# Two more raw weight tiles in a second MLP, an own first order for an attention layer, and a column copy moved three visits on

## The chip, the core and the metric

The kernel runs on one core of a Trainium2 chip. The core's engines work side by side and wait for one another through semaphores: TensorE (PE, matrix multiplies; loading a weight into it is counted apart as PEld), VectorE (DVE), ScalarE (ACT), GpSimd (POOL) and SyncE (SP), which here only issues DMAs. The metric is the device time of one execution in microseconds (us), lower is better.

## What is computed

Two transformer layers on 512 latent tokens and 256 context tokens of width 1024. Layer 0 mixes by differential attention, layer 1 by neighbourhood attention on an 8 x 64 grid plus the context; each is followed by an MLP of width 4096. Both halves of a layer are normed, and shifted, scaled and gated by vectors that come from conditioning vectors through a weight `w_mod`. Cut to what matters here:

```python
for i in range(DEPTH):                       # DEPTH = 2
    mod_l = split(silu(c) @ w_mod[i] + b_mod[i], 6)        # six sections of 1024, for latent tokens
    mod_c = split(silu(c_ctx) @ w_mod[i] + b_mod[i], 6)    # the same for context tokens
    h_l = rms_norm(x, norm1_g[i]) * (1 + mod_l[1]) + mod_l[0]
    h_c = rms_norm(ctx, norm1_g[i]) * (1 + mod_c[1]) + mod_c[0]
    y_l, y_c = mixer_i(h_l, h_c, ...)        # q, k, v projections, attention, output projection
    x = x + mod_l[2] * y_l
    x = x + mod_l[5] * (square(relu((rms_norm(x, norm2_g[i]) * (1 + mod_l[4]) + mod_l[3]) @ w_mlp1[i])) @ w_mlp2[i])
    ...
return x
```

Everything is float32. The last layer updates only the latent tokens.

## The kernel before

**Numbers in two parts.** Each float32 operand of a large product is split into a high part (ACT copies it to a reduced form) and the remainder (POOL or DVE subtracts, L152); a product is three multiplies, high by high, high by low, low by high. A weight is therefore loaded by SP into a raw tile of tag R (512 KB), ACT writes the high half of a tile of tag W from it (L146) and POOL the low half in two cuts (L152). The raw tile is free when both have read it.

**Tiles.** `sbt` (L81) hands out tiles by tag. For a tag in `self.room` it goes round over all places of the pools that are open for the tag: R has two places throughout, and two more are opened for the second MLP (L1208), four in all. There, R also takes the MLP's second weight in blocks (L887), some of which DVE adds or subtracts in place (L927 to L950), since the second MLP product is made of seven block products in place of eight.

**Who sets the order.** A planner places all instructions, at build time, by a clock of its own: an instruction goes to its engine's queue when, by that clock, what it needs is there, and among those that are ready the one that stands first in the program's text goes first. Inside `manual_schedule(engines=PINNED)` PE, SP and POOL (L61) keep the text's order among themselves; DVE and ACT are placed by the planner there too, but for single instructions that are held with `keep_in_program_order`. Each engine then works through its queue in order and waits where an input is not there.

**Layer 1's attention.** Eight groups of two heads. A group's steps are written out as a string of words, which `run` (L1074) goes through: `Q0a` to `Q5b` are halves of the projections of six token tiles (12 multiplies each, L414; tiles 0 and 1 are context), `U0`, `U2`, `U4` turn two tiles' queries and keys (transposes L640, L642), `S`, `T`, `V` are scores, turning and weighting of four units; `w` and `c` load and split the next group's weights; `m` is a visit, below. Marks behind a word (`'`) say that the step belongs to the group one or two back. Group 0 to 6 use CYCLE1 (L47); in group 0 the marked steps fall away, as there is no group behind it. The projections' sums lie in one of three PSUM banks of tag A (PS_ATTN1, L57), which ACT and DVE empty (L421, L626, L627).

**The seam in front of it.** The first MLP ends with `done0` (L1145), called for each of the six token tiles: it stores the tile, and after each odd tile norms the pair (`normed`, L310 to L316) and calls `modulated` (L319): for the eight slices of 128 columns, PE transposes both tiles (L333), ACT scales and shifts (L336), DVE writes the high and the low part (L338, L339) into `hT1`, from which the projections read. This lies outside the pinned region, before it in the text.

**Visits.** A section of the modulation is computed in four visits (`Mods.visit`, L1054; eight times two multiplies at L289, added up by DVE, L291), each with a weight of 1 MB which SP loads one visit ahead. The fourth visit stores the section's rows to DRAM (four ACT DMAs, L1068). For a shift or a scale of a norm (sections 0, 1, 3, 4) the next visit reads them back as columns, with two SP DMAs of 4 KB whose pieces are single numbers (L1060), and DVE writes them into `mB` (L276) or `mA` (L279) in `mod_set`. In the attention of layer 0 (the words of START0, CYCLE0 and END0) and in the first MLP it is the same routine.

## Time and profile before

| what | us |
|---|---|
| time before, median of three runs | 1849.92 (1848.83 to 1850.58) |
| the profiled execution's own time | 1851.53 |
| attention of layer 0, one turn of the written order | about 48 |
| first MLP, about | 558 to 1056 |
| the seam and the first group of layer 1 | 1056 to 1110 |
| attention of layer 1, projections of groups 1 to 7 | 1110 to 1410 |
| second MLP | 1480 to 1850 |

The kernel's page and the answers of its trace show all times from the start of the span. A row of a timeline gives start, duration, engine, line of the kernel, operation, the tiles written and read, how often, and in brackets the idle time in front and what ended it. Five lines of the page that the text below does not show again:

```profile
...
PE   6988999997899999999999988989998989999988
DVE  4677888876666565656559657768776567777685
POOL 3755666643335575766566613334445447878773
PEclk9989999998999999999999989999998989999999
...
PE 65%; DVE 11%; ACT 7%; POOL 6%; issue 5%; DMA 5%; ACTq 0%; SPq 0%; POOLq 0%; DVEq 0%
...
```

The slices are 46 us long each; slices 23 and 24 hold the seam, slices 33 and on the second MLP.

### The profile page before, as it was taken

The page shows a single profiled execution, that of the slowest core. Times are in us where ns is not written, and L with a number is a line of the kernel's source. Part 1 is how long each engine was busy: PE and PEld are TensorE (multiplying, and loading weights), DVE is VectorE, ACT ScalarE, POOL GpSimd, SP SyncE. Part 2 cuts the span into 40 slices and gives each one's busy share as a digit, 9 for nine tenths or more (in the row PEclk, how much of TensorE's full clock was granted, in tenths as well). Part 3 has the DMA queues.
Part 4 walks back from the last instruction along what each step waited for, and adds up shares of the span by engine and source line. Part 5 has one row for each costly group of instructions (what it writes and reads, how often), then busy time and mean ns, then how long its engine had stood idle before and what let it go on. Part 6 is the DMA issues. An engine that isn't in the chain of part 4 may idle for free.

```text
span 1849.7 us, 27540 instructions
## 1 busy us (share of the span) xinstructions
PE 1729.0 (93%) x9918; PEld 1521.2 (82%) x9918; DVE 1265.9 (68%) x2328; ACT 936.8 (51%) x1962; POOL 1046.2 (57%) x1002
## 2 busy tenths in 40 slices
PE   6988999997899999999999988989998989999988
PEld 4878888885788899899988878989897777878767
DVE  4677888876666565656559657768776567777685
ACT  4566776765344343334342446667676344544432
POOL 3755666643335575766566613334445447878773
PEclk9989999998999999999999989999998989999999
DMA  9222222225536644544442333333332333334441
GB/s 336 69 83 78 79 72 85 92 81 186 200 116 177 197 114 111 154 123 119 112 131 80 114 121 119 123 106 112 106 129 98 109 113 125 126 125 148 138 135 69
DMA packets 104809, 227.29 MB, mean 123 GB/s; under 512 B 22160, under 2 KB 38752, under 8 KB 100576
## 3 DMA queue, kind: packets, MB, share of 16 engines
q1 hardware_dynamic: 95152, 212.56, 36.1%
q10 hardware_dynamic: 9520, 12.97, 1.9%
q8 instruction: 78, 1.28, 0.3%
q14 instruction: 59, 0.48, 0.1%
HBM read 207.19 MB, written 18.30 MB: 122 GB/s over the span
## 4 chain that ended last, share of the span: by engine, by line
PE 65%; DVE 11%; ACT 7%; POOL 6%; issue 5%; DMA 5%; ACTq 0%; SPq 0%; POOLq 0%; DVEq 0%
PE PD L851 19%; PE PA L414 14%; PE PB L911 6%; PE PA L911 6%; PE PA L759 4%; POOL W L152 4%; PE PA L992 3%; DMA R<-in_w_dram 3%; PE PS L523 2%; PE PB L558 2%; PE PQ L404 1%; ACT W L146 1%; PE PS L662 1%; PE PB L708 1%; PE PB L693 1%
## 5 line engine op out<-in xcount | busy, mean ns | idle before, releaser
L152 POOL TENSOR_TENSOR W<-R,W 128x512 fp32r<-128x512 f32 x270 | 416.3, 1570 | 162.2 <-ACT W L146 161.4
L851 PE MATMUL PD<-Q,W 128*128 128x384 f32 (+2 forms) x1992 | 379.8, 344 | 11.7 <-DVE Q L339 5.6
L851 PEld LDWEIGHTS PD<-Q,W 128*128 128x128 f32 x1992 | 345.6, 189 | 35.0 <-ACT W L146 7.6
L146 ACT ACTIVATE W<-R 128x1024 fp32r<-128x1024 f32 (+1 forms) x165 | 168.0, 1021 | 189.9 <-DMA R<-in_w_dram 50.4
L152 POOL TENSOR_TENSOR W<-N,W 128x512 fp32r<-128x512 f32 x98 | 141.8, 1468 | 110.1 <-ACT W L146 103.8
L911 PE MATMUL PB<-W,H 128*128 128x512 f32 x738 | 191.9, 395 | 5.5 <-DVE Q L919 4.4
L911 PE MATMUL PA<-W,H 128*128 128x512 f32 x732 | 190.9, 395 | 3.8 <-DVE H L919 2.6
L414 PE MATMUL PA<-W,Q 128*128 128x384 f32 (+1 forms) x1008 | 175.8, 327 | 0.0
L911 PEld LDWEIGHTS PB<-W,H 128*128 128x128 f32 x738 | 139.5, 190 | 36.0 <-DVE Q L919 5.2
L301 POOL TENSOR_TENSOR SQ<-SQ,half 128x4 f32<-128x4 f32 (+1 forms) x96 | 95.3, 994 | 128.3 <-DVE SQ L427 127.1
L911 PEld LDWEIGHTS PA<-W,H 128*128 128x128 f32 x732 | 137.9, 189 | 34.6 <-DVE H L919 3.0
L414 PEld LDWEIGHTS PA<-W,Q 128*128 128x128 f32 x1008 | 159.9, 193 | 0.9
L414 PE MATMUL PA<-WB,H 128*128 128x384 f32 x576 | 108.7, 342 | 2.6 <-DVE Q L475 2.6
L146 ACT ACTIVATE W<-N 128x1024 fp32r<-128x1024 f32 x49 | 51.8, 1058 | 111.5 <-PE PB L911 39.4
L759 PE MATMUL PA<-W,H 128*128 128x512 f32 x384 | 98.5, 407 | 8.3 <-DVE T L764 3.8
L414 PEld LDWEIGHTS PA<-WB,H 128*128 128x128 f32 x576 | 98.7, 189 | 3.5 <-DVE Q L475 3.4
L869 DVE SCALAR_TENSOR_TENSOR H<-N,H 128x512 fp32r<-128x512 f32 (+1 forms) x57 | 67.2, 1181 | 47.1 <-ACT H L868 46.8
L851 PE MATMUL PD<-H,W 128*128 128x512 f32 (+1 forms) x408 | 95.2, 383 | 0.0
L759 PEld LDWEIGHTS PA<-W,H 128*128 128x128 f32 x384 | 72.1, 193 | 26.8 <-DVE T L764 5.9
L529 ACT ACTIVATE E<-PS,SA 128x768 f32<-128x768 f32 (+1 forms) x96 | 72.9, 759 | 40.4 <-DVE SA L528 36.9
L674 POOL TENSOR_SCALAR E<-E,SA 128x256 f32<-128x256 f32 x64 | 59.2, 936 | 55.8 <-DVE SA L671 55.4
L528 DVE TENSOR_REDUCE SA<-PS 128x1 f32<-128x768 f32 (+1 forms) x96 | 74.5, 777 | 21.3 <-ACT E L529 10.8
(265 smaller groups left out, 3540.0 us busy)
## 6 DMA issues: line engine op xcount, KB each, us to landing
R<-in_w_dram SPq DMA_DIRECT2D x121, 512.0 KB
M<-in_wmod_dram SPq DMA_DIRECT2D x32, 1024.0 KB
N<-in_w_dram SPq DMA_DIRECT2D x49, 512.0 KB
R<-in_wqa_dram SPq DMA_DIRECT2D x32, 384.0 KB
R<-in_wqb_dram SPq DMA_DIRECT2D x32, 384.0 KB
C<-in_wmod_dram SPq DMA_DIRECT2D x16, 512.0 KB
M<-in_wmod_dram SPq DMA_DIRECT2D x16, 512.0 KB
Y<-in_rpb_dram SPq DMA_DIRECT2D x48, 128.0 KB
```

Source lines behind the costliest of these rows:

```text
L146: high = nc.scalar.activation(w[:, 0, :n], raw, AF.Copy)
L152: low = (eng or nc.gpsimd).tensor_sub(w[:, 1, o:e], raw[:, o:e], w[:, 0, o:e].bitcast(F32))
L301: nc.gpsimd.tensor_tensor(r, ss, self.half[:, :n], op=ALU.pow)
L414: nc.tensor.matmul(acc[:, :n], hT[kt][:, x, P * i:P * i + P], w[kt // 2][:, y, o:o + n], start=(kt == 0 and p == 0), stop=(kt == KT - 1 an ...
L528: nc.vector.tensor_reduce(mx, s, op=ALU.max, axis=AX, negate=True)
L529: nc.scalar.activation(e[:, m, :nk], s, AF.Exp, bias=mx[:, 0:1], accum_out=sm[:, m:m + 1])
L674: nc.gpsimd.tensor_scalar_mul(e[:, 1, o:o + 256], e[:, 1, o:o + 256], r[:, 1:2])
L759: nc.tensor.matmul(ps, oHL[h][:, x, c:c + P], w[h // 2][:, y, 512 * (h % 2):512 * (h % 2) + 512], start=(first and h == hs[0] and p == 0), ...
L851: nc.tensor.matmul(ps[:, at:at + b1 - b0], w[kt // 4][:, x, o:o + P], hT[kt][:, y, b0:b1], start=(kt == 0 and p == 0), stop=(kt == KT - 1 ...
L869: nc.vector.scalar_tensor_tensor(u[:, 1], src, 1.0, u[:, 0].bitcast(F32), op0=ALU.mult, op1=ALU.subtract)
L911: nc.tensor.matmul(ps, u[:, x, f, P * i:P * i + P], w[:, y, 512 * f:512 * f + 512], start=(f == 0 and p == 0), stop=(f == 1 and p == 2))
L992: nc.tensor.matmul(ps, hd[:, x, P * i - c0:P * i - c0 + P], w[f][:, y, 512 * n:512 * n + 512], start=(f == 0 and p == 0), stop=(f == len(h ...
```

## The change

Three parts, which touch different stages.

- **Six raw tiles.** In the second MLP, tag R goes round over six places: the four of before and two tiles that lie idle there, one of tag C4 and one of tag X (`self.spare`, set once).
- **START1 and N.** `modulated` becomes a generator that stops in front of each further PSUM bank (four banks of two slices for this caller; `modulate` runs it through for the other). For the last pair of `done0` it is not run there; its four steps become the word N in a new order START1, which replaces CYCLE1 for group 0. In START1 the halves of Q0 and Q1 come first, then two N, Q2a, two N; the split `c0` and the load `w2` come after these, and the first visit `m` after Q3a.
- **Columns.** The two reads are issued one visit after the store, as before, into one constant tile `columns`; `mod_set` now stands at the head of the third visit after the store instead of the first.

```diff
--- before.py
+++ after.py
@@ -44,6 +44,7 @@
 END0 = """x0 x1 x2 x3 m S1' O2'' O3'' V4'' T0' U4' X0 V5'' T1' X1 m S2' O4'' X2 x4 V0' n S3' x5 P0a O5'' T2' X3 P1a
 X4 V1' O0' n S4' X5 B0 P0b V2' O1' x6 P1b T3' P2a T4' S5' P2b O2' P3a V3' V4' m P3b T5' P4a O3'
 X6 P4b V5' P5a P5b O4' O5'"""
+START1 = """w0 w1 Q0a Q0b Q1a Q1b N N Q2a N N c0 w2 Q2b U0 Q3a m Q3b c1 w3 Q4a Q4b c2 m U2 Q5a Q5b c3"""
 CYCLE1 = """w0 w1 Q0a m T3'' U4' Q1a c0 w2 V2'' V3'' Q0b S0' Q1b Q2a S1' Q2b Q3a T0' S2' Q4a c1 w3 T1' Q3b S3' V0' U0
 Q4b c2 m U2 Q5a T2' Q5b c3 V1'"""
 LAST1 = """Q0a m T3'' U4' Q1a c0 x0 x1 V2'' V3'' Q0b S0' Q1b X0 x2 Q2a S1' Q2b X1 Q3a T0' S2' Q4a T1' Q3b X2 S3' V0'
@@ -74,6 +75,7 @@
         self.dram = pool("dram", 1, space=DRAM)
         self.flip = 0
         self.room, self.turns, self.last = {"R": [(self.rpool, 2, None)]}, {}, {}
+        self.spare = {}
 
 
     BUFS = {"H": 8, "Q": 8, "E": 2, "X": 2, "Y": 6, "T": 1, "MA": 2, "SQ": 12, "SA": 12, "SO": 8, "C4": 1}
@@ -83,7 +85,10 @@
         if tag in self.room:
             pools = [r[:2] for r in self.room[tag] for _ in range(r[1])]
             k = self.turns[tag] = self.turns.get(tag, -1) + 1
-            pool, bufs = pools[k % len(pools)]
+            k %= len(pools) + len(self.spare.get(tag, ()))
+            if k >= len(pools):
+                return self.spare[tag][k - len(pools)]
+            pool, bufs = pools[k]
         else:
             pool, bufs = self.sb, self.BUFS[tag]
         return pool.tile(shape, dt, tag=tag, name=f"{tag}{self.n}", bufs=bufs)
@@ -197,6 +202,7 @@
 
         self.mA = c.tile([P, 2, 2, KT, 2], F32, name="mA")
         self.mB = c.tile([P, 2, 2, KT, 2], F32, name="mB")
+        self.columns = c.tile([P, KT, 2], F32, name="columns")
         self.rows = self.dram.tile([2, 6, 2, D], F32, name="rows")
 
     def load_layer0(self):
@@ -326,6 +332,8 @@
         bank = None
         for kt in range(KT):
             if kt % per == 0:
+                if kt:
+                    yield
                 bank = self.pst(tag[0], (P, 256 * per))
                 for k in range(kt, min(kt + per, KT)):
                     for j, xn in enumerate(xns):
@@ -337,6 +345,10 @@
                                  scale=self.mA[:, l, norm, kt, s:s + 1])
             nc.vector.tensor_copy(hT[kt][:, 0, cols], f)
             nc.vector.tensor_sub(hT[kt][:, 1, cols], f, hT[kt][:, 0, cols].bitcast(F32))
+
+    def modulate(self, *args):
+        for _ in self.modulated(*args):
+            pass
 
     def normed_early(self, xs):
 
@@ -813,7 +825,7 @@
                         nc.scalar.dma_start(self.x1[i][:, 512 * n:512 * n + 512], xh[i, n])
                 if i % 2 == 1:
                     xns = [self.normed([xh[j, 0], xh[j, 1]]) for j in (i - 1, i)]
-                    self.modulated(xns, (i - 1, i), l, 1, hT, tag_p)
+                    self.modulate(xns, (i - 1, i), l, 1, hT, tag_p)
 
         return dict(weights=weights, begin=begin, fetch=fetch, split=split, step=step, split_last=split_last, end=end)
 
@@ -1037,7 +1049,7 @@
 
 
     def __init__(self, b, todo, halves=()):
-        self.b, self.halves, self.ready, self.back = b, halves, [], []
+        self.b, self.halves, self.ready, self.stored, self.fetched, self.landed = b, halves, [], None, None, None
         self.todo = [(l, sec, v) for l, sec in todo for v in range(4)]
         self.acc = None
 
@@ -1054,12 +1066,12 @@
     def visit(self, bank='A'):
 
         b, nc = self.b, self.b.nc
-        for l, sec in self.back:
-            t = b.sbt('SA', [P, KT, 2])
+        if self.landed:
+            b.mod_set(*self.landed, slice(0, KT), b.columns)
+        self.landed, self.fetched, self.stored = self.fetched, self.stored, None
+        if self.fetched:
             for s in range(2):
-                nc.sync.dma_start(t[:, :, s], b.rows[l, sec, s].rearrange("(k p) -> p k", p=P))
-            b.mod_set(l, sec, slice(0, KT), t)
-        self.back = []
+                nc.sync.dma_start(b.columns[:, :, s], b.rows[(*self.fetched, s)].rearrange("(k p) -> p k", p=P))
         if self.ready:
             l, sec, v, acc, raws = self.ready.pop(0)
             b.mod_visit(acc, v, raws, bank)
@@ -1067,7 +1079,7 @@
                 for q in range(4):
                     nc.scalar.dma_start(b.rows[l, sec, :, 256 * q:256 * q + 256], acc[32 * q:32 * q + 2])
                 if sec in (0, 1, 3, 4):
-                    self.back.append((l, sec))
+                    self.stored = l, sec
         self.load()
 
 
@@ -1148,9 +1160,14 @@
                         nc.scalar.dma_start(b.x2[i - 2][:, 512 * n:512 * n + 512], xh[i, n])
                 if i % 2 == 1:
                     xx = [b.normed([xh[j, 0], xh[j, 1]]) for j in (i - 1, i)]
-                    b.modulated(xx, (i - 1, i), 1, 0, hT1, 'B1')
-
-            w1 = []
+                    steps = b.modulated(xx, (i - 1, i), 1, 0, hT1, 'B1')
+                    if i == NT - 1:
+                        last.append(steps)
+                    else:
+                        for _ in steps:
+                            pass
+
+            w1, last = [], []
 
             units, begun = [b.bias1(u) for u in range(6 * GROUPS1)], []
 
@@ -1191,14 +1208,15 @@
             with tc.manual_schedule(engines=PINNED):
                 own = {"P": lambda n: proj["step"](2 * int(n[0]) + (n[1] == "b")), "B": lambda _: proj["begin"](),
                        "x": lambda n: proj["fetch"](int(n)),
-                       "X": lambda n: proj["split"](int(n), nc.gpsimd), "m": lambda _: late.visit()}
+                       "X": lambda n: proj["split"](int(n), nc.gpsimd), "m": lambda _: late.visit(),
+                       "N": lambda _: next(last[0], None)}
                 for c in range(GROUPS1):
                     if c == GROUPS1 - 1:
                         b.close("W1")
                         b.open("right", W=1, ST=2)
                         proj.update(b.project(1, a["wob"], b.oT1, 2, lambda i: b.x2[i - 2], 'HQ', 'QH', 'S1', done))
                     heads[c] = b.group1(c, w.setdefault(c, []), hT1, split=proj.get("split_last"))
-                    run(CYCLE1 if c < GROUPS1 - 1 else LAST1, c, heads, load, split, **own)
+                    run(START1 if c == 0 else CYCLE1 if c < GROUPS1 - 1 else LAST1, c, heads, load, split, **own)
                 b.close("M", "W1")
                 b.open("left", W=3)
                 run(END1, GROUPS1, heads, load, split, **own)
@@ -1206,6 +1224,7 @@
             xh1, hT3 = done
         b.close("ST")
         b.open("right", R=2)
+        b.spare["R"] = [b.sbt(t, [P, 1024]) for t in ("C4", "X")]
         with b.psum_phase("psD", **PS_MLP1):
 
             def done1(i):
```

## The prediction

> **What bounds the kernel now.** I read the page first, then busy time by stretches (columns: stretch, length, busy us of PE, weight load, DVE, ACT and POOL with counts, granted TensorE clock, DMA share, GB/s), then the chain, then the timelines and waits of the stretches that fell short.
>
> ```profile
> span 1849.7 us, 27540 instructions
> PE 1729.0 (93%) x9918; PEld 1521.2 (82%) x9918; DVE 1265.9 (68%) x2328; ACT 936.8 (51%) x1962; POOL 1046.2 (57%) x1002
> ...
> 1068.20:1116.10 47.90, 39.53 (x249) 35.10 (x249) 26.62 (x76) 20.93 (x53) 9.99 (x16) 0.88 0.39 126
> 1551.00:1592.00 41.00, 41.00 (x180) 33.54 (x179) 29.37 (x34) 19.71 (x26) 33.42 (x23) 1.00 0.42 146
> 1778.00:1792.00 14.00, 8.73 (x24) 5.69 (x25) 14.00 (x15) 3.03 (x4) 11.71 (x8) 0.76 0.34 117
> ```
>
> PE is busy 93% of the span; a gain has to come out of PE's holes, or of the half clock behind them. The change touches three places with holes. At the seam between layer 0's MLP and layer 1's attention, 47.9 us hold 39.53 of PE and the mean clock is 0.88. In the second MLP a middle turn is full (41.00 of 41.00), yet its end (1778 to 1792) has 8.73 of 14.00 at clock 0.76. The third is the attention of layer 1, where the chain passes one same piece (a group's first 24 multiplies) once per turn:
>
> ```profile
> 1122.50 3.53 PE PA L414 x24
> ...
> 1163.17 3.51 PE PA L414 x24
> ...
> 1202.22 3.49 PE PA L414 x24
> ...
> 1247.96 3.53 PE PA L414 x24
> ...
> 1287.07 3.51 PE PA L414 x24
> ...
> 1330.42 3.49 PE PA L414 x24
> ```
>
> The turns last 40.67, 39.05, 45.74, 39.11 and 43.35 us. The turn of 39.05 is the plain one; 45.74 and 43.35 hold the copies of the columns of sections 3 and 4, and 40.67 follows a store of rows that is not copied back.
>
> **The seam: START1 and N.** No instruction is added: 16 transposes (L333), eight activations (L336) and 16 DVE steps (L338, L339) of the last pair go from free placing into PE's fixed order, and the first visit m goes from behind Q0a to behind Q3a, with its SP loads. These are PE's rows, then those of DVE and ACT, in order of time:
>
> ```profile
> 1060.95 0.77 PE L414 MATMUL PA<-H,Q 128*128 128x256 f32 x5
> ...
> 1072.38 1.04 PE L333 MATMUL PB<-ident,N 128*128 128x128 f32 x8
> ...
> 1076.26 0.64 PE L289 MATMUL PA<-M,silu 128*32 128x256 f32 x8 [1.78 <-DMA M<-in_wmod_dram]
> ...
> 1092.69 8.95 PE L414 MATMUL PA<-H,Q 128*128 128x384 f32 x36 [3.81 <-DVE H L627]
> ...
> 1101.62 2.35 PE L414 MATMUL PA<-H,Q 128*128 128x384 f32 x12
> ...
> 1110.09 1.58 PE L414 MATMUL PA<-W,Q 128*128 128x256 f32 x12
> ```
>
> ```profile
> 1076.97 0.42 DVE L291 TENSOR_TENSOR MA<-PA,MA 128x256 f32<-128x256 f32 x1 [1.01 <-PE PA L289]
> ...
> 1079.26 0.88 DVE L316 TENSOR_SCALAR N<-X,SA 128x512 f32<-128x512 f32 x2 [0.73 <-POOL SA L301]
> 1086.24 1.94 ACT L336 ACTIVATE Y<-PB,mB,mA 128x256 f32<-128x256 f32 x4 [10.62 <-PE PB L333]
> ...
> 1090.94 0.28 ACT L421 ACTIVATE Y<-PA 128x128 f32<-128x128 f32 x1
> ```
>
> PE, in fixed order, stood 1.78 at m, for a weight tile still landing. That also kept DVE (L291, 1.01), behind which the norm of the last tile waits; its columns end at 1079.26 + 0.88 = 1080.14. ACT then stood 10.62 on the last pair's transposes, with the evictions of Q0 to Q2 (L421) queued behind it until 1090.94; all three A banks were full, and PE stood 3.81. Both stops go: at its new place m comes after 1085, when its tile is there; and the first two N stand behind Q0 and Q1, so the first evictions are ready before ACT's first L336 is.
>
> What is late next? By 1072.38 + 1.04 = 1073.4 the down products and the transposes before the last pair's are through, and twelve of the 48 multiplies of Q0 and Q1 (the five of the first row, and seven more). The other 36 take 36 x 1.58/12 = 4.7, to 1078.1. The last tile's norm, without L291's 1.01, is done near 1079.1. So PE stands about 1 at the first N, with Q2a and all later PE work behind it. Then come N N, Q2a, N N, Q2b; U0 needs a fourth A bank, the first eviction, which ACT may place behind some L336. I allow 1.5 there: 2.5 of new waits in all. Q4a needs ACT's eight L336 and DVE's halves; Q2b, U0, Q3 and m cover that with over 3 x 2.35 = 7. Without that cover PE would stand for up to 3.9, the eight L336 at 1.94 per four. c0's split stays behind the last L336 on ACT, and w2 behind it on SP; c2, which wants w2, comes five halves, 11.8, later.
>
> The half clock behind the two stops costs as well:
>
> ```profile
> 1076.00:1082.00 6.00, 5.74 (x38) 5.33 (x39) 2.44 (x8) 0.00 (x0) 0.55 (x1) 0.72 0.31 95
> 1090.00:1098.00 8.00, 5.31 (x17) 5.31 (x18) 5.73 (x17) 3.83 (x12) 2.38 (x3) 0.57 0.50 164
> ```
>
> 5.74 x (1 - 0.72) = 1.6 and 5.31 x (1 - 0.57) = 2.3 of PE's work. The gain is 1.78 + 3.81 + 1.6 + 2.3 - 2.5 = **7.0**. Bounds: 12.3 if every hole (47.9 - 39.53 = 8.4) and both losses of clock (3.9) go, and a loss of 2.4 if the new order stands for 4 at the first N, for 4 at U0 and for the 3.9 at Q4a: 9.5 - 11.9.
>
> The Trainium skill, "TensorE: Matmul & The Clock Gate", Part 1, lets the clock fall to half only after an idle window of about 3.4 us. By that rule the stop of 1.78 costs no clock and the gain would be 5.4. The trace differs: 0.72 behind a stop of 1.78. The rows decide.
>
> **Six raw tiles.** Nothing is added; R turns over six places, so a load waits for the sixth tile back, not the fourth. The waits of 1496 to 1803 (total, times, longest), and one such load:
>
> ```profile
> PE PD L851 <- ACT W L146: 5.5, 5, 1.8
> ...
> PE PB L911 <- DVE Q L919: 4.4, 2, 2.7
> ...
> ACT W L146 <- DMA R<-in_w_dram: 39.0, 14, 5.5
> ...
> DVE R L939 <- DMA R<-in_w_dram: 5.0, 1, 5.0
> ```
>
> ```profile
> 1664.96 2.84 SPq L130 DMA_DIRECT2D R<-in_w_dram  x2
> ...
> 1669.99 1.06 ACT L146 ACTIVATE W<-R 128x1024 fp32r<-128x1024 f32 x1 [4.53 <-DMA R<-in_w_dram]
> ```
>
> A load is issued when POOL has finished the tile's former content, and ACT can split it 5.03 us later (1664.96 to 1669.99); PE then stood for the W tile: 5.5 over five turns. Two places more let a load start two splits earlier, four half splits of 33.42/23 = 1.45 or 5.8, more than the longest wait of 1.8. I take 4.5 of the 5.5. At the end, 4.4 of PE's holes come from DVE, which was busy 14.00 of 14.00 after it had itself stood 5.0 for a raw tile (L939); earlier tiles spread that work, but the evictions still come in a burst. I take 2. Sum **6.5**. Bounds: 13.3 if all of 5.5 and 4.4 and the half clock (14 x 0.24 = 3.4) go; 0 if another limit stands right behind; and a loss, the last rival. What is late next is the W tile (four of them) and PE itself.
>
> **The columns three visits on.** The two loads of 4-byte pieces stay on SP one visit after the store; the DVE step (L276 or L279) stands two visits later in the text, on one constant tile. What it cost: the first transposes of tile pair 4, 5 (L640) after a store alone, then after two copies; and SP, DVE around them:
>
> ```profile
> 1156.63 0.33 PE L640 MATMUL PA<-ident,Y 128*128 128x128 f32 x1 [2.12 <-DVE Y L429]
> ...
> 1238.68 0.47 PE L640 MATMUL PA<-ident,Y 128*128 128x128 f32 x1 [4.51 <-DVE Y L429]
> ...
> 1322.33 0.33 PE L640 MATMUL PA<-ident,Y 128*128 128x128 f32 x1 [3.26 <-DVE Y L429]
> ```
>
> ```profile
> 1232.37 1.00 SPq L1060 DMA_DIRECT2D SA<-rows  x2
> ...
> 1234.18 0.69 DVE L695 TENSOR_TENSOR N<-PB,N 128x512 fp32r<-128x512 f32 x1 [0.30 <-ACT N L694]
> ...
> 1237.53 0.17 DVE L276 COPY mB<-SA 128x16 f32<-128x16 f32 x1 [2.66 <-DMA SA<-rows]
> ...
> 1155.55 0.69 DVE L695 TENSOR_TENSOR N<-PB,N 128x512 fp32r<-128x512 f32 x1 [0.34 <-ACT N L694]
> ```
>
> Beyond the store's 2.12, which stays, the copies took 2.39 and 1.14 of PE, and with the clock 45.74 - 40.67 = 5.1 and 43.35 - 40.67 = 2.7. The one of attention 0 that I can frame took 1.1, and I take its twin as alike:
>
> ```profile
> 283.50:331.50 48.00, 46.75 (x321) 43.03 (x320) 38.98 (x94) 34.21 (x99) 30.80 (x43) 1.00 0.25 86
> 331.50:380.60 49.10, 46.42 (x313) 42.18 (x312) 38.22 (x89) 33.73 (x95) 30.23 (x42) 1.00 0.28 92
> ```
>
> So 10 us are there to win. Does the change win them? DVE is not in PINNED: its order comes from the planner's own clock, not from the text. The trace shows that such placing jumps far: five multiplies of Q0a ran at 1060.95, eleven us before transposes (1072.38) of the stage that stands ahead of them in the text. The data landed 5.16 after the issue (1232.37 to 1237.53), while the step sits right behind the first L695 (1234.18): the planner believed it landed about 2 after. That belief is not changed, and nothing but the load holds the step. DVE has a hole just there (0.34 in the turn without a copy, row 1155.55). So I expect the step to **float back to the same place**, with the same wait: 0.
>
> **Sum.** 7 + 6.5 + 0 = 13.5 off. The profiled execution took 1851.53 (span 1849.7 and 1.8 around it), 1.61 above the median of the three runs, 1849.92. On its own time that makes 1838.0; against the median, **1836.4**. With 3 to 10 for each of the two gains its own range is 1830 to 1844.
>
> **Rivals.**
> (1) The step stays where the text has it, on data long landed. For: later in the text, it yields to the second L695 where both are ready, and then to L429, behind which no transposes wait for it. Against: the hole above. It gives 10 more: 1826.4.
> (2) The raw tiles gain nothing, since the W tiles bind next. For: ACT's splits wait for PE's release too. Against: the 39.0 on loads in the rows above. 1836.4 + 6.5 = 1842.9, still faster; if the seam too gives only 3, 1846.9, no change.
> (3) Slower: with raw tiles always at hand POOL splits without pause, and DVE's steps on two tensors of SBUF run against it. Same operation and shape, beside POOL's splits and away from them:
>
> ```profile
> L944 DVE TENSOR_TENSOR N<-N,N 128x512 f32<-128x512 f32 x7 | 12.5, 1786 | 0.0
> ...
> L947 DVE TENSOR_TENSOR N<-N,N 128x512 f32<-128x512 f32 x7 | 4.7, 677 | 0.0
> ```
>
> The price is 1786 - 677 = 1.1 a step. Eleven DVE steps a turn that went from free to blocked, 12.1, would lift DVE from 29.37 to PE's 41; from there it decides. What a turn with a full DVE costs, the last one shows: 4.4 of PE. In the six others too: 1849.92 - 7 + 6 x 4.4 = 1869.3. Against: POOL's work does not grow (33.42 of 41), so neither can the overlap by much. The Trainium skill, "SBUF — State Buffer", calls the port pair that DVE and GpSimd share an exclusive lock which the loser waits out; these two rows agree.
>
> **Chances.** Forecast 0.45, (1) 0.28, (2) 0.17, (3) 0.10. The range 1822 to 1847 holds the first two, with their terms' spread of some 4 below (1), and most of the third. A difference of 0.2% is 3.7 us, about what a measurement tells from no change. Faster: 0.44 + 0.28 + 0.11 = 0.83; the same: 0.01 + 0.06 = 0.07; slower 0.10.
>
> **What would show it.** Right: in 1068 to 1116's counterpart no stop above 2 and one group sooner by 7; PE's waits on L146 under 1 in the second MLP; L276 and L279 still waiting for the columns' load, and turns of about 45 and 43. Wrong: copies' turns near 40.7 (rival 1); ACT's waits for loads gone, but PE's for W as long (2); DVE near 41 a turn (3). What would upset all: the planner orders freely placed work anew everywhere, and a stage that this change doesn't name could move.

## The result, and the profile after

| | before | after |
|---|---|---|
| time, median of 20 runs each (us) | 1850.57 (1846.30 to 1854.28) | 1843.95 (1839.81 to 1850.30) |
| ratio to before, 95% interval | | 0.9964 (0.9955 to 0.9973) |
| span of the profiled execution | 1849.7 | 1844.2 |

The kernel became 6.6 us faster (1850.57 - 1843.95). The sign and the range of the prediction held; its size, 13.5, was double what came.

From the page after, the chain of work that ended last, by engine (share of the span):

```profile
PE 70%; DVE 11%; ACT 6%; DMA 4%; issue 4%; POOL 4%; ACTq 0%; SPq 0%; POOLq 0%; DVEq 0%
```

The chain had 65% on PE before and has 70% now; DMA went from 5% to 4% of it. To see where the rest went I cut both executions at the same work: DVE adds up each of the 40 visits in one step (L291, after the change L297), so the starts of these steps are 40 marks that mean the same in each kernel. The timeline of before, DVE; the first and the last row shown are the 8th and the 21st mark:

```profile
265.73 0.41 DVE L291 TENSOR_TENSOR MA<-PA,MA 128x256 f32<-128x256 f32 x1
...
271.71 0.27 DVE L534 TENSOR_SCALAR SA<-SA,SA,neglam 128x1 f32<-128x1 f32 x1
272.14 0.35 DVE L567 SCALAR_TENSOR_TENSOR O<-O,SO,one 128x128 f32<-128x128 f32 x1 [0.15 <-POOL SO L301]
272.41 1.01 DVE L535 SCALAR_TENSOR_TENSOR E<-E,SA 128x768 f32<-128x768 f32 x1
273.45 0.43 DVE L440 TENSOR_TENSOR Q<-PC,Q 64x256 fp32r<-64x256 f32 x1
273.91 0.35 DVE L562 SCALAR_TENSOR_TENSOR O<-PB,SA,O 128x128 f32<-128x128 f32 x1
274.54 0.17 DVE L276 COPY mB<-SA 128x16 f32<-128x16 f32 x1 [0.28 <-DMA SA<-rows]
...
372.50 0.18 DVE L279 SCALAR_TENSOR_TENSOR mA<-SA,gT 128x16 f32<-128x16 f32 x1 [1.21 <-DMA SA<-rows]
...
569.14 0.41 DVE L291 TENSOR_TENSOR MA<-PA,MA 128x256 f32<-128x256 f32 x1
```

The same of after (L276, L279 and L291 of before are L282, L285 and L297 here; L534 to L567 are 12 higher), with the issue of the two loads on SP and the second copy:

```profile
266.35 0.41 DVE L297 TENSOR_TENSOR MA<-PA,MA 128x256 f32<-128x256 f32 x1
...
271.71 1.02 SPq L1074 DMA_DIRECT2D columns<-rows  x2
...
272.34 0.27 DVE L546 TENSOR_SCALAR SA<-SA,SA,neglam 128x1 f32<-128x1 f32 x1
...
276.53 0.17 DVE L282 COPY mB<-columns 128x16 f32<-128x16 f32 x1 [3.92 <-DMA columns<-rows]
276.62 0.35 DVE L579 SCALAR_TENSOR_TENSOR O<-O,SO,one 128x128 f32<-128x128 f32 x1
...
377.30 0.17 DVE L285 SCALAR_TENSOR_TENSOR mA<-columns,gT 128x16 f32<-128x16 f32 x1 [3.83 <-DMA columns<-rows]
...
578.15 0.41 DVE L297 TENSOR_TENSOR MA<-PA,MA 128x256 f32<-128x256 f32 x1
```

From the 8th to the 21st mark before took 569.14 - 265.73 = 303.4 and after 578.15 - 266.35 = 311.8: attention 0 and its end are **8.4 longer**. The rows show the place. Before, the step that writes the columns (L276) stood behind L567, L535, L440 and L562 and waited 0.28. After, it (L282) stands four instructions earlier, right behind L546 (L534 before), while its load, issued at 271.71, is still on the way; DVE stands 3.92 there, and the four that stood ahead of it now wait behind it. The second copy (L285) waits 3.83, where before (L279) it waited 1.21. The turns with these copies grew by 3.9 and 3.0. The third copy's step moved from the start of the first MLP (558.60, no wait) to 504.44, into the end of attention 0, where it waits 0.84; the piece between the two marks around it grew by 1.5. Together that is the 8.4.

By such cuts, the time of each stage against that of before (us; the marks used are the 8th, 21st, 28th, 33rd and 40th, the last stage ends with the span):

| stage, length before | after - before |
|---|---|
| up to 265.7 | +0.6 |
| attention 0 and its end, 303.4 | +8.4 |
| first MLP, seam, first group of layer 1, 574.8 | -8.9 |
| layer 1, turns without a copy, 89.1 | +1.8 |
| layer 1, both turns with a copy and on, 159.0 | -0.5 |
| end of layer 1 and second MLP, 457.8 | -6.9 |

They add up to the spans' 5.5. Each row is one execution against one, and some rows scatter. In the runs below the first row lies between -1.1 and +2.1. The last row lies between -2.4 and +1.2 in the four runs that change nothing in it (e5, e7, e8, e10), and between -0.3 and -8.1 in the six others that have six raw tiles; so its size has to come from timed runs. Two gains of about the forecast size are there; a loss of 8.4 stands where I had put nothing. PE's waits in the seam, then in the second MLP (what waited for what: us in total, times, longest):

```profile
PE PB L341 <- DVE N L322: 2.2, 1, 2.2
PE PA L295 <- DMA M<-in_wmod_dram: 0.5, 1, 0.5
...
PE PA L923 <- DVE Q L931: 3.1, 1, 3.1
PE PB L923 <- DVE Q L931: 2.0, 1, 2.0
```

In the seam both stops are gone, 3.8 for the A bank and 1.8 at m; what came is 2.2 at the first N and 0.5 at m. In the second MLP the 5.5 on ACT's W tiles are gone, but a stop of 3.1 on an eviction is new. The timelines of DVE and PE around it, then the 10 us around it (PE busy 7.28, clock 0.83):

```profile
1583.02 2.36 DVE L939 TENSOR_TENSOR X<-X,R 128x1024 f32<-128x1024 f32 x1 [4.13 <-DMA X<-in_w_dram]
1585.30 1.27 DVE L931 TENSOR_TENSOR Q<-PA,Q 128x512 f32<-128x512 f32 x2
...
1586.72 2.90 PE L923 MATMUL PA<-W,H 128*128 128x512 f32 x6 [3.13 <-DVE Q L931]
```

```profile
1584.00:1594.00 10.00, 7.28 (x25) 5.91 (x26) 9.30 (x12) 1.38 (x2) 6.67 (x5) 0.83 0.71 240
```

DVE stood 4.13 for a block of the second weight (L939) with PE's evictions (L931) behind it; PE stood 3.13, and the mean clock of this window is 0.83, which on 7.28 us of work is another 1.2.

### The profile page after: what moved, and what is told of

Same layout as the page of the kernel before. It is cut to its first block, busy times and chain, and to the rows that moved or that the text cites. A ratio compares the mean times of both kernels' runs of the same rounds, so it can differ in the third digit from the quotient of the medians.

```text
span 1844.2 us, 27543 instructions
## 1 busy us (share of the span) xinstructions
PE 1730.8 (94%) x9918; PEld 1524.9 (83%) x9918; DVE 1254.8 (68%) x2328; ACT 937.0 (51%) x1962; POOL 1038.6 (56%) x1002
## 4 chain that ended last, share of the span: by engine, by line
PE 70%; DVE 11%; ACT 6%; DMA 4%; issue 4%; POOL 4%; ACTq 0%; SPq 0%; POOLq 0%; DVEq 0%
PE PD L863 21%; PE PA L426 14%; PE PA L923 8%; PE PB L923 8%; PE PA L771 3%; PE PA L1004 3%; POOL W L157 2%; PE PS L535 2%; PE PB L570 2%; PE PQ L416 2%; PE PS L674 1%; PE PB L720 1%; PE PB L705 1%; DMA columns<-rows 1%; ACT E L541 1%
## 5 line engine op out<-in xcount | busy, mean ns | idle before, releaser
L157 POOL TENSOR_TENSOR W<-R,W 128x512 fp32r<-128x512 f32 x214 | 328.3, 1559 | 138.7 <-ACT W L151 128.4
L151 ACT ACTIVATE W<-R 128x1024 fp32r<-128x1024 f32 (+1 forms) x137 | 138.6, 1013 | 130.2 <-POOL W L157 31.6
L541 ACT ACTIVATE E<-PS,SA 128x768 f32<-128x768 f32 (+1 forms) x96 | 72.8, 758 | 40.5 <-DVE SA L540 37.4
L863 PEld LDWEIGHTS PD<-H,W 128*128 128x128 f32 x408 | 75.0, 192 | 15.7 <-DVE H L347 0.8
```

Source lines behind the costliest of these rows:

```text
L151: high = nc.scalar.activation(w[:, 0, :n], raw, AF.Copy)
L157: low = (eng or nc.gpsimd).tensor_sub(w[:, 1, o:e], raw[:, o:e], w[:, 0, o:e].bitcast(F32))
L541: nc.scalar.activation(e[:, m, :nk], s, AF.Exp, bias=mx[:, 0:1], accum_out=sm[:, m:m + 1])
L863: nc.tensor.matmul(ps[:, at:at + b1 - b0], w[kt // 4][:, x, o:o + P], hT[kt][:, y, b0:b1], start=(kt == 0 and p == 0), stop=(kt == KT - 1 ...
```

## The experiments

The theory after this reading: the constant tile, not the later place in the text, let the planner put the step earlier on DVE in attention 0, and that cost 8.4; seam and raw tiles gave what was forecast. The rivals: the later place did it; or the freely placed work of attention 0 was reshuffled by the other two parts; or the turns are long for the loads and not for the step. Ratios are to before, run on the same chip; "us" is the ratio's distance from 1 times 1851; "attention 0" is the stage of that name, against before, in the one profiled execution.

| run | what | ratio (95%) | us | attention 0 |
|---|---|---|---|---|
| | the change | 0.9964 (0.9955 to 0.9973) | -6.7 | +8.4 |
| e1 | without the columns part | 0.9940 (0.9925 to 0.9956) | -11.1 | +1.8 |
| e2 | constant tile, step directly behind the loads | 0.9954 (0.9937 to 0.9970) | -8.5 | +8.1 |
| e3 | SA tile, step three visits on | 0.9927 (0.9911 to 0.9943) | -13.5 | +1.1 |
| e4 | the change, step held | 0.9900 (0.9884 to 0.9916) | -18.5 | -0.2 |
| e5 | columns part alone | 1.0036 (1.0023 to 1.0048) | +6.7 | +5.5 |
| e6 | six raw tiles alone | 0.9965 (0.9955 to 0.9976) | -6.5 | +0.1 |
| e7 | START1 and N alone | 0.9978 (0.9963 to 0.9993) | -4.1 | +0.1 |
| e8 | START1's order without N | 0.9993 (0.9983 to 1.0003) | -1.3 | +0.1 |
| e9 | step three visits on, tile of a tag of its own | 0.9966 (0.9953 to 0.9979) | -6.3 | +3.5 |
| e10 | columns part and hold alone | 0.9957 (0.9946 to 0.9969) | -8.0 | +1.4 |
| e11 | e4 with five raw tiles | 0.9876 (0.9863 to 0.9889) | -23.0 | -0.1 |
| e12 | five raw tiles alone | 0.9922 (0.9903 to 0.9941) | -14.4 | +0.2 |

**e1, the columns part undone.** `visit` is that of before.

```diff
-        if self.landed:
-            b.mod_set(*self.landed, slice(0, KT), b.columns)
...
+        for l, sec in self.back:
+            t = b.sbt('SA', [P, KT, 2])
...
+            b.mod_set(l, sec, slice(0, KT), t)
```

> The changed kernel with the columns part undone: the two loads go into a fresh SA tile and the step stands directly behind them, as before; START1, N and the six raw tiles stay. Theory (the columns part alone costs what is missing, in attention 0): the turns at 235 to 284 and 355 to 406 us lose their 3.8 and 2.95, the end of attention 0 its 1.3, and the kernel takes 7 + 6.5 = 13.5 us less than before, 1836 to 1838 where before takes 1850.5. Rival (the freely placed work was reshuffled by START1 and the raw tiles, and attention 0 pays for that): 1844, as the changed kernel.

The ratio's interval, 8.1 to 13.9 us less than before, takes in the theory's 13.5 and not the change's 6.7. Attention 0 lost all but 1.8 of its excess: the rival that START1 and the raw tiles reshuffled it falls.

**e2 and e3, tile against place.** e2 keeps the constant tile and puts the step back behind its loads; e3 keeps the step three visits on and puts the loads into an SA tile.

```diff
 e2
-        if self.landed:
-            b.mod_set(*self.landed, slice(0, KT), b.columns)
...
+            b.mod_set(*self.fetched, slice(0, KT), b.columns)
 e3
-                nc.sync.dma_start(b.columns[:, :, s], ...)
+            self.t = b.sbt('SA', [P, KT, 2])
+                nc.sync.dma_start(self.t[:, :, s], ...)
```

> The changed kernel, but the step stands directly behind its two loads in the text again; only the tile that they go into is the constant one. Theory (the constant tile moved the step, its later place in the text did nothing): DVE stands 3.9 and 3.8 us at the two copies of attention 0, and the time is that of the changed kernel, 1843 to 1845. Rival (the later place in the text moved it): 1836 to 1838, and DVE stands 0.3 and 1.2 there as before.

> The changed kernel with the step three visits on, but on a fresh SA tile in place of the constant one. Theory (the constant tile is what moved the step): DVE stands 0.3 and 1.2 us at the two copies of attention 0, as before, the turns there are as before, and the time is 1836 to 1838. Rival (the later place in the text): 1843 to 1845.

The timeline of DVE in e2:

```profile
271.57 0.27 DVE L546 TENSOR_SCALAR SA<-SA,SA,neglam 128x1 f32<-128x1 f32 x1
...
275.96 0.17 DVE L282 COPY mB<-columns 128x16 f32<-128x16 f32 x1 [4.12 <-DMA columns<-rows]
```

and in e3:

```profile
275.43 0.35 DVE L574 SCALAR_TENSOR_TENSOR O<-PB,SA,O 128x128 f32<-128x128 f32 x1
277.57 0.17 DVE L282 COPY mB<-SA 128x16 f32<-128x16 f32 x1 [1.79 <-DMA SA<-rows]
```

With the constant tile the step sits right behind L546 even where the text has it directly behind its loads; with an SA tile it sits behind L574 (before's L562), as before, even three visits on. The later place alone (in the text it is two visits behind that of before) moved nothing here. Attention 0 is 8.1 longer in e2 and 1.1 in e3. e3's time is that of the forecast, 13.5 less than before. The two intervals of time overlap a little (0.9937 to 0.9943), so the timings alone would not quite separate them; the rows do.

**e9, what about the tile.** The step of e3, but the fresh tile comes from a tag of its own with two places, CO, so that nothing holds its place when the loads are to be written.

```diff
-    BUFS = {..., "SO": 8, "C4": 1}
+    BUFS = {..., "SO": 8, "C4": 1, "CO": 2}
...
+            self.t = b.sbt('CO', [P, KT, 2])
```

> The changed kernel with the step three visits on and a fresh tile for each copy, but on a tag of its own (CO, two places) in place of the constant tile or an SA tile. It tells what about the constant tile moved the step. Theory (an SA place has to be given back by an earlier reader before the loads may be written into it, and that hold, in the planner's clock, kept the loads and so the step later; a place that nothing holds lets it go early): DVE stands about 4 us at both copies of attention 0 and the stage ends about 8 later, as with the constant tile; ratio 0.995 to 0.9965. Rival (it is the tile being constant, not fresh): as with the SA tile, attention 0 about 1 longer than before, ratio 0.9927.

The timeline of DVE in e9:

```profile
272.22 0.28 DVE L546 TENSOR_SCALAR SA<-SA,SA,neglam 128x1 f32<-128x1 f32 x1
...
275.01 0.17 DVE L282 COPY mB<-CO 128x16 f32<-128x16 f32 x1 [2.52 <-DMA CO<-rows]
```

Right behind L546 again: it isn't that the tile is constant, it is that its place is free. In the traces of before and e3, the first of the two loads waits for a semaphore of an ACT step that reads an SA tile (L529, in e3 L541), by which the SA place is given back; in those of after, e2 and e9 it has no such wait at the first copy. On the chip that wait costs nothing visible: SP issues the loads at 271.02 before and at 271.71 after, when the stage was 0.6 late already. So it would have to act in the planner's clock, where it makes the load, and so the step, late; that last link is argued, not shown. The excess of attention 0 was smaller than expected, 3.5 and not 8; DVE stood 2.52 and, at the second copy, 3.29. The stage of attention 0 in e2, then in e9, length and PE's busy time first:

```profile
265.59:577.11 311.52, 284.21 (x1771) 245.90 (x1770) 221.81 (x498) 172.43 (x460) 142.74 (x181) 0.96 0.37 125
266.23:573.11 306.88, 279.42 (x1771) 240.29 (x1770) 223.16 (x498) 171.97 (x460) 143.53 (x181) 0.98 0.38 127
```

PE's idle time is alike, 27.3 and 27.5 (24.1 before, 29.0 after); what differs is the busy time for the same multiplies, 284.21 at a clock of 0.96 and 279.42 at 0.98. The ratio, 0.9966, came out at the edge of the expected range.

**e4, the step held.** One addition: the step may not go ahead of the DVE instruction in front of it in the text.

```diff
-            b.mod_set(*self.landed, slice(0, KT), b.columns)
+            b.tc.keep_in_program_order(b.mod_set(*self.landed, slice(0, KT), b.columns))
```

> The changed kernel with one addition: the step is kept behind the DVE instruction that stands ahead of it in the text, so that it cannot float up from its third visit. Theory (each us that DVE stands for the columns costs PE about one in attention 0 and 1): the waits of 3.9, 3.8 and 0.8 in attention 0 and those of layer 1 go, the turns of layer 1 that hold a copy fall from about 45 and 43 to about 41, and the time is 1844 - 8 - 8 = 1828, with 1826 to 1831 as its range. Rival (the turns are long for another reason, such as the loads themselves on the queues): the waits go and the time stays above 1836.

The timeline of DVE, two marks of a turn of layer 1 with a copy, before:

```profile
1232.99 0.42 DVE L291 TENSOR_TENSOR MA<-PA,MA 128x256 f32<-128x256 f32 x1
...
1269.37 0.41 DVE L291 TENSOR_TENSOR MA<-PA,MA 128x256 f32<-128x256 f32 x1
```

The same two marks in e4, and the step of that copy:

```profile
1225.04 0.42 DVE L297 TENSOR_TENSOR MA<-PA,MA 128x256 f32<-128x256 f32 x1
...
1257.84 0.41 DVE L297 TENSOR_TENSOR MA<-PA,MA 128x256 f32<-128x256 f32 x1
...
1267.74 0.17 DVE L282 COPY mB<-columns 128x16 f32<-128x16 f32 x1
```

The row of the step carries no wait, nor does that of any other copy; attention 0 is as long as before, and the piece of layer 1's turn between these two marks takes 1257.84 - 1225.04 = 32.8, where before had 36.4. The loads themselves are still issued at the same visit, so it was the standing step that cost, not the loads. Ratio 0.9900: 18.5 less than before, a little less than the 22 expected (1850 - 1828), with an interval of 15.5 to 21.5. Against the change, the hold alone is worth 11.8 (18.5 - 6.7).

**e5, e6, e7, the parts alone,** each put into the kernel before by itself, with no other line changed.

```diff
 e5
+        if self.landed:
+            b.mod_set(*self.landed, slice(0, KT), b.columns)
+        self.landed, self.fetched, self.stored = self.fetched, self.stored, None
...
 e6
+        b.spare["R"] = [b.sbt(t, [P, 1024]) for t in ("C4", "X")]
...
 e7
+                    if i == NT - 1:
+                        last.append(steps)
...
+                    run(START1 if c == 0 else CYCLE1 if c < GROUPS1 - 1 else LAST1, c, heads, load, split, **own)
```

> The kernel before with the columns part alone; its order and its raw tiles are those of before. Theory (the constant tile puts the step into an earlier hole of DVE, whatever else is in the kernel): DVE stands about 4 us at each of the two copies of attention 0, that stage ends 7 to 8.5 us later than before, and the kernel is slower than before by that much, ratio 1.004 to 1.005. Rival (the loss needs the other two parts): within 0.1% of before.

> The kernel before with the six raw tiles alone. Theory: nothing changes up to the second MLP, which gets 4.5 us from PE's waits for W tiles and 2 from its tail, 6.5 in all: ratio 0.9965. Rival (the tail depends on how DVE's freely placed work falls, as where the columns part was undone and the stage from 1384 us gained 2.1 in its profile and not 6.9): 2 to 3 us, ratio 0.9985, with PE's waits on L146's tile gone and its holes in the tail as before.

> The kernel before with START1 and N alone. Theory: nothing changes up to 1060 us, the first group of layer 1 ends 8.4 to 9 sooner, the next turn is 1.5 longer, and 7 stay: ratio 0.9962. Rival (freely placed work of attention 0 or of the first MLP falls otherwise and takes some of it): under 4.

e5 is 6.7 slower (4.3 to 8.9): the loss needs neither of the other parts. DVE stood 2.37 and 3.66 at the two copies, where about 4 each were expected, and attention 0 grew by 5.5, where 7 to 8.5 were expected. Its profiled execution, 1852.80, is among the fastest of its twelve (median 1857.38), and its whole span is only 1.3 above that of before; so the 6.7 rests on the timed runs.

e6 is 6.5 faster (4.4 to 8.3), the forecast's size. Its profiled execution is the slowest of its twelve (1850.94, median 1844.62), and its last stage is only 0.3 shorter. That stage before, then in e6:

```profile
1391.96:1849.73 457.77, 423.00 (x1906) 345.17 (x1906) 312.77 (x415) 200.53 (x306) 301.40 (x219) 0.96 0.35 119
1391.73:1849.16 457.43, 425.89 (x1906) 348.06 (x1906) 304.56 (x415) 201.52 (x306) 300.00 (x219) 0.96 0.35 119
```

PE's idle time did fall, from 34.8 to 31.5, but PE was busy 2.9 longer with the same multiplies. So a single profile is used here for waits and not for the sum; the last section shows one thing that can make executions differ.

e7 is 4.1 faster (1.3 to 6.8), while its trace shows 8.2 gained up to the first group's end, 1.6 given back in the turns after that, and 2.5 more gained in the turns with a copy, which this part doesn't touch. The 7 expected lie just outside the timed interval.

**e8, the order without N.** START1 with N doing nothing; the last pair's four steps run outside the ordered region, as before.

```diff
-                    if i == NT - 1:
-                        last.append(steps)
...
+                    for _ in steps:
+                        pass
...
+                       "N": lambda _: None})
```

> The order START1 alone: the visit m stands behind Q3a and the loads and splits where START1 has them, but the last pair's four transposing steps are left outside the ordered region, ahead of it in the text, as before. Theory (two causes of about equal size): the stop of PE at m and its half clock go, 1.8 + 1.6, and the stop for the banks of A with its half clock stays, 3.8 + 2.3: 3.4 us less than before, ratio 0.998. Rival A (m's early place made the bank stop too, since DVE and the last tile's norm stood behind it): 7, as with N. Rival B (N does it all): 0 to 1.

PE's longest wait in the seam of e8:

```profile
PE PA L653 <- ACT sq L436: 5.4, 1, 5.4
```

The stop for the A bank was not kept but moved: PE now stood 5.4 at U0, for ACT's squares (L436). In this execution the stage with the seam was 5.0 shorter and the next turns 1.6 longer, 3.4 net, the number of the theory of two causes. But PE's idle time in that stage fell only from 14.5 to 13.6, against 10.9 in e7; the rest of the 5.0 is shorter busy time with the same multiplies. Timed, e8 takes 1.3 less (0.6 more to 3.1 less): that holds rival B's 0 to 1, and 3.4 lies just outside. So the order alone gains little, and N is needed. Whether N would do it without m's new place was not run.

**e10, hold and columns alone,** in the kernel before.

```diff
+        if self.landed:
+            b.tc.keep_in_program_order(b.mod_set(*self.landed, slice(0, KT), b.columns))
```

> The kernel before with the columns part and the hold, but with before's order and four raw tiles. Theory (the waits that went with the hold cost what they cost, independent of the rest): attention 0 as long as before, the two turns of layer 1 with a copy 3.6 and 2.6 shorter, nothing else: 6 less than before, ratio 0.9967. Rival (with the old order the turns of layer 1 have another limit): under 2.

8.0 less (5.7 to 10.0), and the stage with layer 1's copies is 6.1 shorter in the trace. The gain of the hold needs neither the new order nor the raw tiles.

**e11 and e12, five raw tiles.** e11 is e4 with tag C4's tile alone added; e12 is the kernel before with the same.

```diff
-        b.spare["R"] = [b.sbt(t, [P, 1024]) for t in ("C4", "X")]
+        b.spare["R"] = [b.sbt(t, [P, 1024]) for t in ("C4",)]
```

> The held version with five raw tiles in the second MLP in place of six (only the tile of tag C4 is added). Theory (a load that starts one split, 2.9 us, earlier already covers PE's longest wait for a W tile, 1.8): PE's waits for ACT's W tile stay away and the time is that of six, within 0.15%. Rival (six are needed, since the second weight's blocks hold places longer): 2 to 4 us more than with six, with waits of PE on L151's tile back.

> The kernel before with five raw tiles in the second MLP (tag C4's tile alone added), nothing else changed. Theory (six places let DVE's first block step stand 4.1 us for a load that lands late, with evictions behind it, so that PE stands 3.1 at half clock; five do not): PE's waits on ACT's W tile go as with six, the stop of 3.1 and its 1.7 us of clock do not come, and the time is 6.5 + 4.8 = 11 us less than before, ratio 0.994. Rival (the gain of five in the held version came from how its freely placed work fell): as with six alone, ratio 0.9965.

What I expected of e11, no difference, did not come: its last stage is 15.0 shorter than before's, that of e4 with six tiles 6.0. The timed intervals of e4 and e11 still touch (0.9884 to 0.9889). e12 and e6, whose intervals lie apart, settle that it is the number of tiles and not the hold: 14.4 less than before (10.9 to 18.0), where six alone give 6.5 (4.4 to 8.3). PE's and DVE's waits in e6 (six):

```profile
PE PA L922 <- DVE Q L930: 3.0, 1, 3.0
PE PB L922 <- DVE Q L930: 2.5, 2, 1.7
...
DVE R L950 <- DMA R<-in_w_dram: 7.9, 1, 7.9
```

and in e12 (five), with ACT's on the loads last:

```profile
PE PB L922 <- DVE Q L930: 1.0, 2, 0.6
...
DVE R L950 <- DMA R<-in_w_dram: 2.2, 1, 2.2
...
ACT W L151 <- DMA R<-in_w_dram: 7.7, 3, 3.0
```

Both have lost PE's waits on W tiles. With six, DVE's block steps stand up to 7.9 for loads, and once PE stands 3.0 behind one; with five the longest is 2.2, PE has no such stop and its evictions' waits at the end fall from 2.5 to 1.0. ACT waits a little for loads again (7.7, where before had 39.0), and PE has no wait on a W tile. Over the last stage PE's idle time is 34.8 before, 31.5 in e6 and 25.9 in e12. Why the planner places the block steps nearer to their data with five is not shown.

**The fastest version** is e11, the change with five raw tiles and the step held: 1828.14 us (1824.37 to 1829.73), 0.9876 of before, against 0.9964 for the change.

## Why the prediction was off

- **The step that failed is the third, "So I expect the step to float back to the same place, with the same wait: 0".** It rested on "nothing but the load holds the step". By e2, e3 and e9 it is the tile that moved the step: the SA place held the load too, and with a tile whose place is free that hold went (how it acts in the planner's clock is argued, not shown). In layer 1 the sentence was right: the waits there are 2.45 and 1.21 (before 2.66 and 1.23) and the stage moved by -0.5. In attention 0 the step went four DVE instructions ahead, waited 3.92 and 3.83, and the stage took 8.4 longer; by e5, the part by itself costs 6.7 (4.3 to 8.9). I had looked at the later place, the part of the edit that the words of the change name, and priced the new tile at nothing. The prediction's last sentence said that freely placed work could move elsewhere, but gave that no price. The second mistake was to look at the copies of attention 0 only for what they cost before, 1.1 each: their small waits (0.28 and 1.21) were small because four DVE instructions stood in front of the step and covered the load, and that cover could be lost.
- **The seam:** 7.0 said; the trace has 8.9 gained and 1.8 given back in the turns behind it. The two stops went and new waits of 2.2 + 0.5 came where I had allowed 2.5. What I counted as gone and was not is some of the clock:

```profile
1086.00:1092.00 6.00, 4.23 (x18) 4.23 (x19) 4.90 (x19) 2.85 (x9) 2.20 (x3) 0.72 0.02 4
```

  The new stop of 2.2 at the first N lies in this window, and 4.23 of PE's work at 0.72 lost 1.2. The Trainium skill, "TensorE: Matmul & The Clock Gate", Part 1, lets the clock fall after an idle window of about 3.4 us, and so would leave it alone here; as in the prediction, the row disagrees. The part alone, timed, came to 4.1 (1.3 to 6.8), so 7 is a little more than the timing allows.
- **The raw tiles:** 6.5 said, 6.5 timed alone (4.4 to 8.3), but as the sum of other terms. The waits on W went in full, 5.5 and not 4.5, and the evictions' waits at the end fell from 4.4 to 2.0. Against that stands what I didn't see: 3.1 + 1.2 for DVE's block step that now waited in front of evictions. These terms add up to 5.5 + 2.4 - 3.1 - 1.2 = 3.6 and not to 6.5; what makes up the rest is open, and that the total came out as forecast is luck. I priced the tiles by who waits for a raw tile (ACT), and not by DVE, whose steps on the same tag are placed anew. With five tiles (e12) the rows show no such stop and the gain is 14.4, more than double; that the stop accounts for all of the difference is not shown.
- **Rival (1),** the step on data long landed, 10 more: the change doesn't do this, but e4 does, by a hold. It won 6.0 in layer 1 (7.8 said) and 0.2 in attention 0 (2.2 said) against before.
- **Rival (2)** is refuted: PE's waits on W did not stay. Its time, 1842.9, came near the measured 1843.95 for another reason. **Rival (3)** is refuted too; DVE had less to do in the second MLP, not more. Before, then after, 150 us each:

```profile
1592.00:1742.00 150.00, 146.82 (x637) 118.99 (x635) 105.74 (x122) 67.93 (x90) 115.35 (x77) 1.00 0.42 137
1594.20:1744.20 150.00, 150.00 (x657) 123.00 (x656) 101.74 (x126) 70.88 (x93) 118.50 (x78) 1.00 0.40 130
```

  DVE is busy 101.74 of 150 after and 105.74 before, while PE is busy 150.00 and 146.82.
- **The range** held, since it reached up to the cases in which half of the gains are missing, and 0.83 had been given to faster. e3, START1 and N with six raw tiles and no new tile, is the kernel that I had forecast. It took 1837.87, 13.5 less than before by its ratio (10.6 to 16.5). That it is just the forecast 13.5 is partly luck, since its two parts alone give 4.1 and 6.5.

## What to carry to other kernels

Where a scheduler places instructions by a clock of its own, look at a tile as a wait too: here, exchanging a rotating tile for one whose place is free let the step go four instructions earlier, in front of work that had covered its load. A step that must not wait is held explicitly; a later place in the text alone moved nothing here. More buffers are to be tried one at a time: the fifth raw tile gave 14.4 us and six gave 6.5, and with six another engine's steps on the same tag stood longer for their data.

## What the hardware showed beside that

The two loads of columns, 4 KB each in pieces of 4 bytes, landed between 3.5 us (before: issue 271.02, step 274.54) and 4.8 us (after: 271.71 to 276.53) after the issue, with the same work around them.

What a stop of PE costs in clock depended on where it fell in time. The granted clock drops to 0.50 for stretches of 3.41 us, one or several in a row, and within one execution their starts lie whole multiples of 3.41 us apart. In the turn of layer 1 at 1154 us PE stands 2.12, before and after alike (L640, after the change L652). Two such pieces of time around it, before:

```profile
1152.57:1155.98 3.41, 1.95 (x26) 1.21 (x15) 2.68 (x6) 2.33 (x5) 2.00 (x4) 1.00 0.77 227
1155.98:1159.39 3.41, 2.76 (x24) 2.76 (x25) 1.56 (x4) 1.19 (x3) 1.62 (x4) 1.00 0.55 196
```

and after:

```profile
1153.23:1156.64 3.41, 1.47 (x16) 1.08 (x10) 2.65 (x6) 2.10 (x5) 2.31 (x5) 1.00 0.81 244
1156.64:1160.05 3.41, 3.23 (x15) 3.24 (x16) 1.15 (x4) 1.31 (x3) 1.17 (x3) 0.50 0.48 179
```

Before, the stop is spread over two pieces and costs no clock. After, most of it lies in one piece, PE is busy only 1.47 of 3.41 there, and the next piece runs at half clock, which costs 3.23 x 0.50 = 1.6. In the fourteen traces, from 90 us on, each piece at full clock with less than 1.5 us of PE's work was followed by one at half clock, and none with more than 2.1 was. So a stop of some 2 us costs no clock or up to half of a piece, 1.7, by where it falls among these pieces, and they lie differently in before and in after. That this is also why executions of one kernel scatter is likely, but not shown, since each kernel has one profile. A forecast has to give the clock behind such a stop a range.
